# A decoder block whose FFN takes a plain product first: pair order, roots and scaling moved

## The chip, the cores and the metric

One core of a Trainium2 chip runs the whole kernel. The core has five engines with a queue each: TensorE (PE, matmuls), VectorE (DVE), ScalarE (ACT), GpSimd (POOL) and SyncE (SP), which issues most of the DMA transfers. Each engine takes its instructions strictly in the order of its queue and waits at semaphores for the others. The metric is the device time of one execution in microseconds (us), the median of several runs.

## The reference

The kernel computes one hybrid decoder block on a sequence of 1024 rows with 1024 columns in float32: a state-space branch and an attention branch, merged and multiplied by `w_o`, and then a gated FFN. The change touches the end of this and all of the FFN:

```python
merged = (jax.nn.sigmoid(gate_a) * y_a + jax.nn.sigmoid(gate_b) * y_b) @ w_o[l]
x = x + g1 * merged

h = modulate(rmsnorm(x, norm2_g[l]), sh2, sc2)
ffn = (jax.nn.silu(h @ w_ffn_gate[l]) * (h @ w_ffn_up[l])) @ w_ffn_down[l]
x = x + g2 * ffn
return rmsnorm(x, norm_f_g)
```

`rmsnorm` multiplies a row by one over the root of its mean square plus 1e-6. The hidden width of the FFN is 2816, that is 22 blocks of 128 or 11 pairs of blocks. The row g2 comes out of a small product of the conditioning vector with `w_ada`.

## The kernel before, in words

**Products.** A float32 product is made of three faster matmuls. Each operand is split into a rounded high part and the rest: `operand` (L462) copies it on ACT with a cast (L473, `wh`) and subtracts on DVE (L474, `wl`), and PE multiplies high by high, high by low and low by high (`PRODUCTS`). Where an operand is a sum of two blocks, the sum comes first (L471), on POOL or DVE. `pieces` makes the right operands of the FFN, out of the activations, and `next_ring` gives the slots of the left ones.

**The output projection, the norm and the transposes** (`attend_out`). For each of eight row tiles PE makes the product with `w_o`, DVE adds x, ACT sums the squares (L1148), `rstd` (L478 on) makes the root, ACT multiplies by it, and PE transposes (L1158) into four blocks of activations b11, b21 (row tiles 0 to 3) and b12, b22 (row tiles 4 to 7). `rstd` goes to and fro between two engines: a scale on DVE (L483), Ln and Exp on ACT (L486, L487), then a correction step in three DVE operations (L489, L493, L494), all on 128x1 elements.

**Gate and up** (`gate_up`, one call for each of the 11 pairs of hidden blocks). Each pair treats the gate weights and the up weights as two-by-two blocks and makes them by seven products instead of eight, in the order `ORDER = (2, 4, 5, 3, 1, 6, 7)`, one product of 12 matmuls for gate and one for up: 7 x 2 x 12 = 168 matmuls (L1255). Product 7 of the seven, for example, needs a sum of two weight blocks and the sum of b21 and b22. The right operands (seven of them, two tiles each) are made during pair 0 and kept. `combine` takes each product out of PSUM into four tiles `C` in slots `f1`: a copy on ACT for products 2 and 5 (L1262, L1266), adds on DVE for the others. PSUM has eight banks of 512 columns, named `tq`, `mm` and `wo` in the profile. At the end of a pair ACT applies Silu (L1235), DVE multiplies (L1236), and POOL makes five sums of the result (L1246), the left operands of the next product, which are stored to `hD` in DRAM. Product 2 of pair 1 is computed early, in the middle of pair 0 (the constant `N2`). Pair 10 goes last, and its result is stored as it is, in `lD`.

**Down** (`down`). Pairs 0 to 9 of the hidden blocks go through the seven-product form again, in three steps of four, three and three pairs (`STEPS`). For each step `weights` loads tiles of `w_ffn_down` into slots `pa` and POOL multiplies each by the row g2 (L1308). Then for each of the seven products the hidden sums are read back from `hD`, POOL adds two weight blocks (L1337), ACT and DVE split (L1334, L1335, L1338, L1339), PE multiplies (L1354), and DVE adds to seven accumulators `acc` (L1360). Four of these accumulators begin with blocks of x, and `acc[7]` is first corrected by `acc[5]` and `acc[4]`, four POOL operations (L1298) at the start of down. In the last step `closing` (L1315) sums the accumulators on POOL into the four result blocks. The two hidden blocks of pair 10 are multiplied last, plainly (L1394, 96 matmuls), and `close` makes the final norm of each row tile and stores it: squares on ACT (L1404, L1398), `rstd`, and a product of row, root and norm weight on DVE (L1379).

**What sets the order.** The program is written in order of the mathematics, with the waits put in by a framework that also sorts the instructions of every queue by its own estimate of when they can run. So the order on a queue is that of the built program and not always that of the text. A tile is a slot in a pool with a fixed number of buffers; a new tile waits until all who read the old one in its slot have done so. Calls of `after` fix one instruction behind another on the same engine, to keep ACT functions of one table together.

## Time and profile before

| what | us |
|---|---|
| median of 3 runs | 1496.89 (1492.9 to 1497.25) |
| the profiled execution | 1498.89 |
| its span, first to last instruction | 1497.2 |
| PE busy | 1414.6 |
| DVE busy | 1125.6 |
| ACT busy | 621.6 |
| POOL busy | 504.3 |

The mean granted clock of PE is 0.976 of full speed. A row of a timeline begins with its start and its length in us; x7 after it says that seven instructions alike stand in it. A bracket at its end gives how long the engine stood idle before it and who released it. In a group's row the busy time is followed by the mean of one in ns. Matmuls overlap: one of 512 columns is shown as 0.39 us, but they follow each other more closely than that.

### The profile page before, as it was taken

To read this page: it belongs to the slowest core of one execution; us is meant where nothing else is said; L and a number is where in the kernel's file an instruction comes from. 1 tells how busy PE (TensorE), PEld (TensorE's weight loads), DVE (VectorE), ACT (ScalarE), POOL (GpSimd) and SP (SyncE) were. 2 spreads that over 40 slices of the span, in tenths; PEclk is the share of its full clock that TensorE was granted. 3 is DMA by queue.
4 is the path that set the end of the run, shared out by engine and by line. 5 is a ranking of instruction groups with operands and counts; after the bars stand their busy time and mean duration, and the time that the engine had idled before them with its cause. 6 is when DMAs were issued, how large, how long until landed. Compare 5 with 4: busy or idle time off the path is not lost.

```text
span 1497.2 us, 18257 instructions
## 1 busy us (share of the span) xinstructions
PE 1414.6 (94%) x6706; PEld 1118.1 (75%) x6706; DVE 1125.6 (75%) x1523; ACT 621.6 (42%) x804; POOL 504.3 (34%) x266
## 2 busy tenths in 40 slices
PE   5898999999999999999998799999999998999995
PEld 3678888787666666668887588888888886888774
DVE  5878995456797989868637866666666669999997
ACT  3321122632587776764236433333333333433323
POOL 1000000102111111104300245444555468888795
PEclk9999999999999999999999899999999999999998
DMA  9556665579011112136533233333333346455312
GB/s 340 134 110 163 151 175 134 158 258 333 27 49 50 35 37 77 50 106 218 183 108 107 81 106 106 106 106 106 106 106 106 106 174 220 143 160 175 100 50 113
DMA packets 180409, 193.55 MB, mean 129 GB/s; under 512 B 28636, under 2 KB 130080, under 8 KB 180320
## 3 DMA queue, kind: packets, MB, share of 16 engines
q1 hardware_dynamic: 171184, 184.86, 39.3%
q10 hardware_dynamic: 8912, 7.48, 1.8%
q8 instruction: 53, 0.87, 0.2%
q14 instruction: 36, 0.29, 0.1%
q0 software_dynamic: 224, 0.05, 0.0%
HBM read 142.40 MB, written 48.76 MB: 128 GB/s over the span
## 4 chain that ended last, share of the span: by engine, by line
PE 61%; DVE 20%; issue 6%; DMA 5%; ACT 4%; POOL 3%; SPq 0%; DVEq 0%; ACTq 0%; POOLq 0%
PE tq L1255 11%; PE mm L1255 5%; PE wo L1255 5%; PE mx L807 5%; PE mm L807 4%; PE ga L733 4%; PE tq L1354 3%; PE acc L807 2%; PE mm L1112 2%; PE mm L641 2%; DMA aw<-in_w_ada_dram 2%; PE z L807 2%; PE wo L1112 2%; PE mm L733 2%; PE tq L1112 1%
## 5 line engine op out<-in xcount | busy, mean ns | idle before, releaser
L471 POOL TENSOR_TENSOR ws<-wb 128x1024 f32<-128x1024 f32 x26 | 64.2, 2470 | 181.1 <-PE tq L1158 78.1
L455 POOL TENSOR_TENSOR wl<-ws,wh 128x1024 fp32r<-128x1024 f32 x12 | 31.2, 2601 | 161.2 <-ACT wh L452 151.8
L900 DVE TENSOR_TENSOR wa<-wa,acc 128x512 f32<-128x512 f32 (+1 forms) x80 | 47.0, 628 | 32.6 <-ACT row L898 30.2
L1308 POOL TENSOR_TENSOR pa<-pa,row 128x1024 f32<-128x1024 f32 x22 | 64.1, 2939 | 2.2 <-DMA pa<-in_w_ffn_down_dram 2.2
L294 POOL MEMSET tz<- 128x1024 f32 x4 | 3.8, 953 | 179.4 <-PE mm L641 96.7
L1246 POOL TENSOR_TENSOR f<-f,f 128x512 f32<-128x512 f32 x30 | 50.0, 1693 | 31.4 <-DVE f L1236 22.9
L872 ACT ACTIVATE ws<-wa 128x1024 f32<-128x1024 f32 (+1 forms) x40 | 39.1, 976 | 48.5 <-DVE wa L869 43.3
L471 POOL TENSOR_TENSOR wgs<-wb 128x1024 f32<-128x1024 f32 x14 | 34.6, 2474 | 72.4 <-DVE wgl L474 30.3
L877 DVE TENSOR_TENSOR wl<-ws,wh 128x1024 fp32r<-128x1024 f32 (+1 forms) x40 | 57.1, 1427 | 1.0
L977 DVE SCALAR_TENSOR_TENSOR acc<-aw,cond,acc 128x512 f32<-128x512 f32 x56 | 43.8, 782 | 7.8 <-DMA aw<-in_w_ada_dram 6.9
L875 DVE SCALAR_TENSOR_TENSOR ws<-wa,ws 128x1024 f32<-128x1024 f32 (+1 forms) x40 | 45.5, 1136 | 4.9 <-ACT ws L874 3.9
L1354 PE MATMUL tq<-f,f 128*128 128x512 f32 x156 | 48.2, 390 | 0.2 <-DVE f L1339 0.2
L1235 ACT ACTIVATE f<-f 128x1024 f32<-128x1024 f32 x22 | 23.3, 1061 | 59.8 <-DVE f L1277 30.4
L903 ACT ACTIVATE wa<-wa 128x1024 f32<-128x1024 f32 (+1 forms) x40 | 38.8, 971 | 19.5 <-DVE wa L900 18.5
L452 ACT CAST wh<-ws 128x1024 fp32r<-128x1024 f32 x24 | 25.1, 1048 | 50.7 <-PE wo L1112 24.0
L807 PE MATMUL z<-q,k 64*128 64x512 f32 (+3 forms) x192 | 42.6, 534 | 3.7 <-DVE wa L869 2.6
L1337 POOL TENSOR_TENSOR wb<-pa 128x512 f32<-128x512 f32 x23 | 40.6, 1776 | 15.7 <-DVE wxl L1335 5.5
L454 POOL TENSOR_SCALAR wh<-ws 128x1024 fp32r<-128x1024 f32 x6 | 7.4, 1238 | 105.2 <-issue 36.1
L1246 POOL TENSOR_TENSOR f<-f 128x512 f32<-128x512 f32 x20 | 42.2, 2127 | 0.0
L807 PE MATMUL mm<-wa,V 128*64 128x512 f32 (+3 forms) x192 | 39.8, 507 | 0.0
L873 ACT ACTIVATE ws<-ws 128x1024 f32<-128x1024 f32 (+1 forms) x40 | 39.0, 974 | 1.1
L874 ACT ACTIVATE ws<-ws 128x1024 f32<-128x1024 f32 (+1 forms) x40 | 38.7, 968 | 0.3
(911 smaller groups left out, 4712.3 us busy)
## 6 DMA issues: line engine op xcount, KB each, us to landing
aw<-in_w_ada_dram SPq DMA_DIRECT2D x64, 256.0 KB, 4.6
hD<-f SPq DMA_DIRECT2D x30, 512.0 KB, 2.8
ws<-in_w_in_dram SPq DMA_DIRECT2D x23, 512.0 KB, 4.9
wb<-in_w_ffn_gate_dram SPq DMA_DIRECT2D x44, 256.0 KB, 4.2
wb<-in_w_ffn_up_dram SPq DMA_DIRECT2D x44, 256.0 KB, 4.5
pa<-in_w_ffn_down_dram SPq DMA_DIRECT2D x22, 512.0 KB, 5.1
wb<-hD SPq DMA_DIRECT2D x40, 256.0 KB, 2.8
x<-in_x_dram SPq DMA_DIRECT2D x16, 512.0 KB, 7.2
```

The lines of the kernel that those rows point to most:

```text
L471: (add or nc.gpsimd).tensor_tensor(st, a, b, op)
L733: self.nc.tensor.matmul(ps, lhsT=w[a][:, k], rhs=act[h][k][:, b], start=(j == 0), stop=(j == n - 1))
L807: return self.tc.keep_in_program_order(self.nc.tensor.matmul(*args, **kw))
L875: nc.vector.scalar_tensor_tensor(st, a, 0.0, st, ALU.max, ALU.add)
L877: nc.vector.tensor_tensor(lt, st, ht.bitcast(F32), ALU.subtract)
L900: nc.vector.tensor_tensor(a[:, x, 0:f], a[:, x, 0:f], r[:, x, 0:f], ALU.subtract)
L977: nc.vector.scalar_tensor_tensor(acc, w[:, j], cj, acc, ALU.mult, ALU.add)
L1112: self.nc.tensor.matmul(ps, lhsT=mg[t // 4][k][:, a, P * (t % 4):P * (t % 4) + P], rhs=ws[k // 2][b][:, k % 2], start=k + j == 0, stop=k + ...
L1246: nc.gpsimd.tensor_tensor(o, a, b, op)
L1255: self.nc.tensor.matmul(ps, lhsT=w[x][:, q, k], rhs=self.B[i](y, k), start=(j == 0), stop=(j == 11))
L1308: nc.gpsimd.tensor_tensor(w, w, g2, ALU.mult)
L1354: nc.tensor.matmul(ps, lhsT=o[x][:, P * t:P * t + P], rhs=o[y][:, R], start=(j == 0), stop=(j == 3 * np_ - 1))
```

## The change

1. Pair 10 is computed first instead of last, by the new function `plain`: an ordinary product with eight block products for each of gate and up, 192 matmuls. It uses b11 and b21 for row tiles 0 to 3, then b12 and b22 for 4 to 7, each as it is. `gate_up` then runs for ten pairs, and the early product of pair 1 is gone.
2. The roots of the second norm and of the final norm are made on ACT alone, by the new function `rstd_s`: Ln, Exp, two operations with a scale and a bias, two multiplications, all 128x1. A tile `eps` holds the constants.
3. The first eight tiles of `w_ffn_down` (`SCALED`) are loaded in the calls of pairs 2 to 9, multiplied by g2 on POOL, and stored in `wD`; `down` reads them from there in its first step. For this the row g2 is made after pair 1 instead of after pair 8.
4. The first step of down takes its products in the order `FIRST`, and the correction of `acc[7]` is issued when two products' operands have been issued.
5. `eps` has 19 columns where three are used, so that the tiles behind it begin at the same offset modulo 256 bytes as before.

The core of the diff:

```diff
-N2 = 3
+SCALED = 8
+FIRST = (2, 3, 1, 6, 7, 5, 4)
...
+    def rstd_s(self, ss, y, h, b=None):
+        act = self.nc.scalar.activation
+        b, bh = b or (self.eps[:, 0:1], self.eps[:, 1:2])
+        self.after(act(y, ss, AF.Ln, bias=b, scale=1.0 / 1024.0), self.fence)
+        self.root = act(y, y, AF.Exp, scale=-0.5)
+        act(h, ss, AF.Identity, bias=bh, scale=-0.5 / 1024.0)
+        self.nc.scalar.mul(h, h, y)
+        act(h, h, AF.Identity, bias=self.eps[:, 2:3], scale=y)
+        self.nc.scalar.mul(y, y, h)
         return y
...
+        self.eps = const.tile([P, 19], F32, name="eps")
+        for n, x in enumerate((1e-6, -0.5e-6, 1.5)):
+            self.after(nc.gpsimd.memset(self.eps[:, n:n + 1], x), self.fence)
...
-                r = self.rstd(const, ss, 1)
+                r = self.rstd_s(ss, *(const.tile([P, 1], F32, name=n, bufs=2) for n in ("r2", "h2")))
...
-                    self.B = {2: self.pieces(2, b11, None, self.PA, "pa"), 4: self.pieces(4, b21, b11, self.PA, "pa")}
+                    self.B = {2: self.pieces(2, b11, None, self.PA, "pa")}
+                    self.b21 = self.pieces(2, b21, None, self.PA, "pa")
...
-        for j in range(11):
+        w_v = i["w_ffn_down"][0].rearrange("(m p) n -> m p n", p=P)
+        self.plain(10, wv)
+        for j in range(10):
             self.gate_up(j, wv, tp)
-            if j == 8:
+            if j == 1:
                 g2 = self.rp.tile([P, 1024], F32, name="row")
                 self.ada_row(g2, 6, tp, self.banks, ("ft", None))
+            if 2 <= j < SCALED + 2:
+                t = tp.tile([P, 1024], F32, name="ft")
+                nc.sync.dma_start(out=t, in_=w_v[j - 2])
+                nc.gpsimd.tensor_tensor(t, t, g2, ALU.mult)
+                nc.sync.dma_start(out=self.wD[j - 2], in_=t)
+            if j == 8:
                 gf = tp.tile([P, 1024], F32, name="gf", bufs=1)
                 nc.scalar.dma_start(out=gf, in_=i["norm_f_g"].partition_broadcast(P))
         self.exp_ln(*self.silus)
         self.down(const, tp, g2, gf)
+    def plain(self, pair, wv):
+        nc = self.nc
+        b11, b12, b21, b22 = self.blocks
+        flat = lambda t: t.rearrange("p q k n -> p (q k n)")
+        w = {}
+        for x in range(2):
+            for y in range(2):
+                t = self.W.tile([P, 2, 4, P], F32, name="wb")
+                for q in range(2):
+                    nc.sync.dma_start(out=t[:, q], in_=wv[q][:, 4 * y:4 * y + 4, 256 * pair + P * x:256 * pair + P * x + P])
+                w[x, y] = [o.rearrange("p (q k n) -> p q k n", q=2, k=4) for o in self.operand(flat(t))]
+        parts = self.B[2], self.b21
+        us = [self.X.tile([P, 1024], F32, name="x1") for _ in range(2)]
+        for h in range(2):
+            if h:
+                parts = self.pieces(2, b12, None, self.PB, "pb"), self.pieces(5, b22, None, self.PB, "pb")
+                self.B[5] = parts[1]
+            for x in range(2):
+                ps = [self.banks.tile([P, 512], F32) for _ in range(2)]
+                for q in range(2):
+                    j = 0
+                    for y in range(2):
+                        for k in range(4):
+                            for a, b in PRODUCTS:
+                                nc.tensor.matmul(ps[q], lhsT=w[x, y][a][:, q, k], rhs=parts[y](b, k), start=j == 0, stop=j == 23)
+                                j += 1
+                g = self.X.tile([P, 1024], F32, name="x1")[:, 0:512]
+                self.after(nc.scalar.activation(g, ps[0], AF.Silu), self.root)
+                nc.vector.tensor_tensor(us[x][:, 512 * h:512 * h + 512], ps[1], g, ALU.mult)
+        for x in range(2):
+            nc.sync.dma_start(out=self.lD[x], in_=us[x])
...
-            if pair == 0 and n > 1:
+            if i not in self.B:
                 b11, b12, b21, b22 = self.blocks
-                if i not in self.B:
-                    u, v, pool, tag = {5: (b22, None, self.PB, "pb"), 3: (b12, b22, self.PB, "pb"), 1: (b11, b22, self.X, "x1"),
-                                       6: (b11, b12, self.X, "x1"), 7: (b21, b22, self.F, "f0")}[i]
-                    self.B[i] = self.pieces(i, u, v, pool, tag, Turns((tp, "ft")))
-            tiles = None
-            if pair == 0 and n < 2:
-                tiles = tuple(self.X.tile([P, 1024], F32R, name="x1") for _ in range(2))
-            if pair == 0 and n == N2:
-                raw = [self.X.tile([P, 2, 4, P], F32, name="x1") for _ in range(2)]
-                for y in range(2):
-                    for q in range(2):
-                        nc.sync.dma_start(out=raw[y][:, q], in_=wv[q][:, 4 * y:4 * y + 4, 256 + P:512])
-                w = self.operand(flat(raw[0]), flat(raw[1]), SIGN_A[2], tuple(self.X.tile([P, 1024], F32R, name="x1") for _ in range(2)),
-                                 nc.vector, nc.vector)
-                w = [t.rearrange("p (q k n) -> p q k n", q=2, k=4) for t in w]
-                self.M2 = tp.tile([P, 2, 512], F32, name="gf", bufs=1)
-                for q in range(2):
-                    ps = self.banks.tile([P, 512], F32)
-                    self.seven(ps, w, q, 2)
-                    nc.scalar.copy(self.M2[:, q], ps)
-            if pair == 1 and i == 2:
-                for q in range(2):
-                    M[q][2] = self.M2[:, q]
-                    self.combine(2, M[q], [None, None, None, C[q][1][:, 512:1024]])
-                continue
+                u, v, pool, tag = {4: (b21, b11, self.PA, "pa"), 3: (b12, b22, self.PB, "pb"), 1: (b11, b22, self.X, "x1"),
+                                   6: (b11, b12, self.X, "x1"), 7: (b21, b22, self.F, "f0")}[i]
+                self.B[i] = self.pieces(i, u, v, pool, tag, Turns((tp, "ft")))
             a, b = TERMS_A[i]
-            w = self.operand(flat(A[a]), b and flat(A[b]), SIGN_A[i], tiles, *(nc.vector if pair == 0 or (i, e) in AENG else nc.gpsimd for e in range(2)))
+            w = self.operand(flat(A[a]), b and flat(A[b]), SIGN_A[i], None, *(nc.vector if pair == 0 or (i, e) in AENG else nc.gpsimd for e in range(2)))
             w = [t.rearrange("p (q k n) -> p q k n", q=2, k=4) for t in w]
             for q in range(2):
                 ps = M[q][i] = self.banks.tile([P, 512], F32)
                 self.seven(ps, w, q, i)
                 self.combine(i, M[q], [C[q][0][:, 0:512], C[q][0][:, 512:1024], C[q][1][:, 0:512], C[q][1][:, 512:1024]])
-        if pair < 10:
-            self.silus = []
+        self.silus = []
...
-        for i, op in ((5, ALU.add), (4, ALU.subtract)):
-            for a in range(2):
-                nc.gpsimd.tensor_tensor(flat(acc[7][a]), flat(acc[7][a]), flat(acc[i][a]), op)
...
-            nc.sync.dma_start(out=w, in_=w_v[m])
-            nc.gpsimd.tensor_tensor(w, w, g2, ALU.mult)
+            if m < SCALED:
+                nc.sync.dma_start(out=w, in_=self.wD[m])
+            else:
+                nc.sync.dma_start(out=w, in_=w_v[m])
+                nc.gpsimd.tensor_tensor(w, w, g2, ALU.mult)
...
-            for n, i in enumerate(ORDER):
+            for n, i in enumerate(ORDER if s else FIRST):
+                if s == 0 and n == 2:
+                    for z, op in ((5, ALU.add), (4, ALU.subtract)):
+                        for a in range(2):
+                            nc.gpsimd.tensor_tensor(flat(acc[7][a]), flat(acc[7][a]), flat(acc[z][a]), op)
...
-                r = self.rstd(const, ss[:, 1:2], 1, ss[:, 0:1], at(t))
+                r = self.rstd_s(ss[:, 1:2], small[:, t, 2:3], small[:, t, 3:4], (small[:, t, 4:5], small[:, t, 5:6]))
-            r = self.rstd(const, ss[:, 0:1], 1, None, at(t))
+            r = self.rstd_s(ss[:, 0:1], small[:, t, 2:3], small[:, t, 3:4])
...
+                        for n, f in ((4, 1.0), (5, -0.5)):
+                            nc.scalar.activation(small[:, t, n:n + 1], ss[:, 0:1], AF.Identity, bias=self.eps[:, n - 4:n - 3], scale=f / 1024.0)
```

On PE's queue, where the output projection ends and gate and up begin (`x_6811`, `x_6939` and `wh`, `wl` are split weights, `pa` a right operand made of b11, `ident` the matrix for transposes); before:

```order
L1255 MATMUL wo<-pa,x_6812 128x512
L1255 MATMUL wo<-pa,x_6811 128x512
L1158 MATMUL tq<-ident,xh 128x128 x6
L1255 MATMUL wo<-pa,x_6811 128x512
L1255 MATMUL wo<-pa,x_6812 128x512
L1255 MATMUL mm<-pa,x_6939 128x512 x2
L1255 MATMUL wo<-pa,x_6939 128x512 x2
L1255 MATMUL mm<-pa,x_6940 128x512
```

and now:

```order
L1228 MATMUL wo<-pa,wh 128x512 x2
L1167 MATMUL tq<-ident,xh 128x128 x6
L1228 MATMUL wo<-pa,wl 128x512
L1228 MATMUL wo<-pa,wh 128x512 x2
L1228 MATMUL wo<-pa,wl 128x512
L1228 MATMUL wo<-pa,wh 128x512 x2
L1167 MATMUL tq<-ident,xh 128x128 x2
L1228 MATMUL wo<-pa,wl 128x512
L1228 MATMUL wo<-pa,wh 128x512 x2
```

The recursive product 2 of pair 0 and the early product behind it have given way to the plain product, whose weights lie in the ring's slots `wh` and `wl` instead of slots of x.

On POOL's queue, in pairs 1 to 4 (`ws<-wb` and `wgs<-wb` are sums of weight blocks, `f_...` the five sums of a pair's result); before:

```order
L471 TENSOR_TENSOR ws<-wb 128x1024 x2
L471 TENSOR_TENSOR wgs<-wb 128x1024
L471 TENSOR_TENSOR ws<-wb 128x1024
L1246 TENSOR_TENSOR f_7410<-f_7412,f_7413 128x512 x2
L1246 TENSOR_TENSOR f_7411<-f_7412,f_7413 128x512
L1246 TENSOR_TENSOR f_7412<-f_7412 128x512
L1246 TENSOR_TENSOR f_7413<-f_7413 128x512
L471 TENSOR_TENSOR wgs<-wb 128x1024
```

and now:

```order
L1270 TENSOR_TENSOR f_7389<-f_7391,f_7392 128x512 x2
L1270 TENSOR_TENSOR f_7390<-f_7391,f_7392 128x512
L1195 TENSOR_TENSOR ft<-ft,row 128x1024 x2
L472 TENSOR_TENSOR wgs<-wb 128x1024
L1270 TENSOR_TENSOR f_7391<-f_7391 128x512
L1270 TENSOR_TENSOR f_7392<-f_7392 128x512
L1195 TENSOR_TENSOR ft<-ft,row 128x1024
L472 TENSOR_TENSOR wgs<-wb 128x1024
L472 TENSOR_TENSOR ws<-wb 128x1024
L1195 TENSOR_TENSOR ft<-ft,row 128x1024
L472 TENSOR_TENSOR ws<-wb 128x1024
L1195 TENSOR_TENSOR ft<-ft,row 128x1024 x2
```

The rows of L1195 are the scaling multiplies. All eight stand within some 15 rows, from the middle of pair 1's five sums on, among the weight sums of the next two pairs, though the text issues one for each of pairs 2 to 9. On SP's queue their loads (L1194) and stores (L1196) stand there in turn, between weight loads of a pair and stores of sums:

```order
L1194 DMA ft<-in_w_ffn_down_dram 128x1024
L1273 DMA hD<-f_7392 128x1024
L1196 DMA wD<-ft 128x1024
L1194 DMA ft<-in_w_ffn_down_dram 128x1024
L1196 DMA wD<-ft 128x1024
L1243 DMA wb<-in_w_ffn_gate_dram 128x4x128
L1243 DMA wb<-in_w_ffn_up_dram 128x4x128
L1194 DMA ft<-in_w_ffn_down_dram 128x1024
L1196 DMA wD<-ft 128x1024
L1194 DMA ft<-in_w_ffn_down_dram 128x1024
```

Before, only weight loads and stores of sums stood on SP's queue in the pairs.

On POOL's queue, from the last of the gate and up pairs into down (`pa<-pa,row` is a multiply by g2, `pb<-pb` the correction, the rows into `ws`, `wgs`, `wb` from `pa` are sums of down weights); before:

```order
L1246 TENSOR_TENSOR f_9311<-f_9313,f_9314 128x512 x2
L1246 TENSOR_TENSOR f_9312<-f_9313,f_9314 128x512
L1246 TENSOR_TENSOR f_9313<-f_9313 128x512
L1246 TENSOR_TENSOR f_9314<-f_9314 128x512
L1308 TENSOR_TENSOR pa<-pa,row 128x1024 x4
L1337 TENSOR_TENSOR ws<-pa 128x512 x2
L1308 TENSOR_TENSOR pa<-pa,row 128x1024 x4
L1337 TENSOR_TENSOR wgs<-pa 128x512
L1337 TENSOR_TENSOR wb<-pa 128x512
L1298 TENSOR_TENSOR pb<-pb 128x1024 x4
L1337 TENSOR_TENSOR wgs<-pa 128x512
```

and now:

```order
L1364 TENSOR_TENSOR ws<-pa 128x512 x2
L1364 TENSOR_TENSOR wgs<-pa 128x512
L1364 TENSOR_TENSOR wb<-pa 128x512 x2
L1351 TENSOR_TENSOR pb<-pb 128x1024
L1364 TENSOR_TENSOR wb<-pa 128x512
L1351 TENSOR_TENSOR pb<-pb 128x1024 x2
L1364 TENSOR_TENSOR ws<-pa 128x512
L1351 TENSOR_TENSOR pb<-pb 128x1024
L1270 TENSOR_TENSOR f_9587<-f_9589,f_9590 128x512 x2
L1270 TENSOR_TENSOR f_9588<-f_9589,f_9590 128x512
L1364 TENSOR_TENSOR wb<-pa 128x512
L1364 TENSOR_TENSOR ws<-pa 128x512
```

The multiplies no longer stand here. The correction is threaded among the weight sums of the first products, and the five sums of pair 9 follow behind it.

More of the change, by code (lines that the diff above doesn't have):

```diff
@@ L475, in operand, with rstd @@
         return h, l
-    def rstd(self, pool, ss, n, more=None, at=None):
+    def rstd(self, pool, ss, n):
         nc = self.nc
-        v = at("v") if at else pool.tile([P, n], F32, name="rv")
-        y = at("y") if at else pool.tile([P, n], F32, name="ry")
-        a = at("a") if at else pool.tile([P, n], F32, name="ra")
-        nc.vector.tensor_scalar(v, ss if more is None else more, 1.0 / 1024.0, 1e-6, ALU.mult, ALU.add)
-        if more is not None:
-            nc.vector.scalar_tensor_tensor(v, ss, 1.0 / 1024.0, v, ALU.mult, ALU.add)
+        v, y, a = (pool.tile([P, n], F32, name=x) for x in ("rv", "ry", "ra"))
+        nc.vector.tensor_scalar(v, ss, 1.0 / 1024.0, 1e-6, ALU.mult, ALU.add)
         self.after(nc.scalar.activation(y, v, AF.Ln), self.fence)
         nc.scalar.activation(y, y, AF.Exp, scale=-0.5)
-        if n == 1:
-            nc.vector.scalar_tensor_tensor(a, y, v, y, ALU.mult, ALU.mult)
-        else:
-            nc.vector.tensor_tensor(a, y, y, ALU.mult)
-            nc.vector.tensor_tensor(a, a, v, ALU.mult)
+        nc.vector.tensor_tensor(a, y, y, ALU.mult)
+        nc.vector.tensor_tensor(a, a, v, ALU.mult)
         nc.vector.tensor_scalar(a, a, -0.5, 1.5, ALU.mult, ALU.add)
         nc.vector.tensor_tensor(y, y, a, ALU.mult)
+        return y
+    def rstd_s(self, ss, y, h, b=None):
[7 more added lines that the diff above has]
+        self.nc.scalar.mul(y, y, h)
         return y
@@ L1236, in gate_up @@
             nc.vector.tensor_tensor(u, u, g, ALU.mult)
-            if pair == 10:
-                nc.sync.dma_start(out=self.lD[x], in_=u)
-        if pair == 10:
-            return
         L, R = slice(0, 512), slice(512, 1024)
```

5 lines of the change are left out of this document (2 added, 3 removed).

## The prediction

> **What bounds the kernel now.** I read the page first, then the busy time by stretches, then PE's waits, and last the timelines around the two places where PE loses time.
>
> ```profile
> PE 1414.6 (94%) x6706; PEld 1118.1 (75%) x6706; DVE 1125.6 (75%) x1523; ACT 621.6 (42%) x804; POOL 504.3 (34%) x266
> PE 61%; DVE 20%; issue 6%; DMA 5%; ACT 4%; POOL 3%; SPq 0%; DVEq 0%; ACTq 0%; POOLq 0%
> ```
>
> The first line is busy time by engine, the second the chain of work that ended last. The kernel is PE-bound, and whatever PE does not lose cannot be won, unless the change removes matmuls. DVE's 20% of the chain says that it is DVE that makes PE wait where it waits. The next view has one row a stretch: its length, then each engine's busy time and instructions, the granted clock, the DMA share.
>
> ```profile
> 690.00:800.00 110.00, 110.00 (x509) 91.48 (x508) 61.83 (x87) 42.06 (x69) 25.79 (x13) 0.98 0.44 153
> 800.00:820.00 20.00, 15.73 (x75) 12.28 (x74) 20.00 (x26) 13.05 (x20) 0.00 (x0) 0.91 0.23 80
> 840.00:862.00 22.00, 11.92 (x41) 9.27 (x40) 22.00 (x23) 10.13 (x12) 3.20 (x1) 0.69 0.16 48
> 880.00:1160.00 280.00, 280.00 (x1237) 231.86 (x1236) 174.14 (x193) 86.40 (x98) 144.38 (x70) 1.00 0.33 107
> 1240.00:1260.00 20.00, 15.74 (x69) 12.35 (x67) 18.96 (x13) 4.47 (x7) 20.00 (x9) 1.00 0.61 223
> 1260.00:1280.00 20.00, 17.97 (x69) 14.69 (x70) 19.89 (x16) 12.94 (x19) 13.13 (x7) 0.83 0.43 141
> 1280.00:1300.00 20.00, 19.24 (x85) 15.60 (x85) 19.63 (x20) 6.86 (x7) 13.66 (x8) 1.00 0.56 175
> 1300.00:1360.00 60.00, 60.00 (x267) 49.69 (x266) 56.96 (x45) 24.28 (x32) 49.25 (x23) 1.00 0.47 142
> ```
>
> Columns of busy time are PE, weight load, DVE, ACT, POOL. Before 800 and from 880 to 1160 PE is full; at 800-820 and 840-862 DVE is full and PE starves, at 1240-1280 DVE and POOL are nearly full together and PE starves again. These PE rows mark the ends of the stages:
>
> ```profile
> 808.90 1.75 PE L1255 MATMUL wo<-pa,x 128*128 128x512 f32 x7
> 876.70 0.61 PE L1255 MATMUL wo<-pa,wh 128*128 128x512 f32 x2
> 1176.82 0.62 PE L1255 MATMUL wo<-pa,wh 128*128 128x512 f32 x2
> 1253.00 0.39 PE L1354 MATMUL tq<-wh 128*128 128x512 f32 x1
> 1480.38 0.39 PE L1394 MATMUL wo<-wh,wl 128*128 128x512 f32 x1
> ```
>
> They are the first gate/up matmul, the first of pair 1, the first of pair 9, the first down matmul and the last matmul. Pairs 9 and 10 are 336 matmuls in 1253.00 - 1176.82 = 76.18 us, so an undisturbed matmul costs 0.2267 us and a pair 38.1 us. From 808.90 to 876.70 PE did 168 matmuls of pair 0 and 24 of the early product of pair 1: 192 x 0.2267 = 43.5 us in 67.8, so 24.3 us went elsewhere (some of it the last transposes). From 1253.00 to 1480.77 it did 936: 212.2 us in 227.8, so 15.6 were lost. These 40 us and the 16.4 us from PE's end to the span's end are all that can be won.
>
> ```profile
> PE tq L1255 <- ACT f L1262: 10.1, 1, 10.1
> PE mm L1255 <- ACT x L473: 2.9, 1, 2.9
> PE mm L1255 <- DVE x L474: 1.4, 1, 1.4
> 852.43 2.35 DVE L471 TENSOR_TENSOR ft<-f,f 128x1024 f32<-128x1024 f32 x2
> 854.80 1.22 PE L1255 MATMUL tq<-pb,wh 128*128 128x512 f32 x2 [10.08 <-ACT f L1262]
> ```
>
> The 10.1 us stall is named after ScalarE's first result copy (L1262), but ScalarE is late itself: its target is an `f1` slot whose old content, the activations b21 and b22, DVE still reads for product 7's operand, as the last thing of its queue (the adds from 852.43 to 854.78). Eight PSUM banks fill meanwhile, PE stops, and two matmuls then take 1.22 us: the granted clock of that stretch is 0.69. So the stall is DVE's whole burst of making seven right operands, priced at 10.1 us of standing and some more of slow clock.
>
> **The plain pair first, and the roots.** The plain product needs no sums of activation blocks, only casts and differences (b11, b21, then b12, b22), and gives DVE 192 matmuls of cover before the first recursive pair asks for more. It costs 24 matmuls more than a pair of seven products: 24 x 0.2267 = +5.4 us, on the critical path. The early product of pair 1 goes; its 24 matmuls return in their own pair, at no cost. What is left of the 24.3 us is the question. Its first part lies with the roots:
>
> ```profile
> 811.88 0.14 DVE L483 TENSOR_SCALAR rv<-ss 128x1 f32<-128x1 f32 x1
> 815.42 0.20 ACT L487 ACTIVATE ry<-ry 128x1 f32<-128x1 f32 x1
> 818.28 0.22 DVE L489 SCALAR_TENSOR_TENSOR ra<-ry,rv 128x1 f32<-128x1 f32 x1
> 821.94 0.16 DVE L494 TENSOR_TENSOR ry<-ry,ra 128x1 f32<-128x1 f32 x1
> ```
>
> One 128x1 root takes from 811.88 to 822.10, 10.2 us for some 1.2 us of work, because each of its four DVE steps queues behind full-size operations. On ScalarE alone it is six operations near 0.2 us, some 1.4 us, threaded among the casts of one queue that is not full (13.05 of 20 us), and I let the last transposes come some 6 us earlier. From the queues I work out by hand, for the changed start: 1.4 us until the first weight cast, whose slot the output projection gives back only at its last matmul, 0.8 for the matching difference, 0.3 for the next, 2 for the transposes of the last two row tiles, then about 2.4 of slow clock and transposing: 6.9 us lost in place of 24.3. The plain pair and pair 0 then end at 808.9 + 360 x 0.2267 + 6.9 = 897.4; nine pairs (342.8) and the four small matmuls of the g2 row (0.9) end gate and up at 1241.1, against 1253.0: **-11.9**. Bounds: if only 3 us are lost, 24.3 - 5.4 - 3 = 15.9 gained; if only the 10.1 us stall goes, 10.1 - 5.4 = 4.7 gained. I stay nearer the first: pair 0's copies find their `f1` slots free some 4 to 8 us early by my count, since b21 and b22 are read during the plain pair.
>
> **Scaling during the pairs.** Eight multiplies leave the start of down:
>
> ```profile
> 1225.36 10.45 POOL L1308 TENSOR_TENSOR pa<-pa,row 128x1024 f32<-128x1024 f32 x4
> 1239.26 10.38 POOL L1308 TENSOR_TENSOR pa<-pa,row 128x1024 f32<-128x1024 f32 x4
> 1252.99 11.23 POOL L1298 TENSOR_TENSOR pb<-pb 128x1024 f32<-128x1024 f32 x4
> 987.80 4.71 POOL L1246 TENSOR_TENSOR f<-f,f 128x512 f32<-128x512 f32 x3 [1.90 <-DVE f L1236]
> L471 POOL TENSOR_TENSOR ws<-wb 128x1024 f32<-128x1024 f32 x21 | 50.4, 2401 | 85.8 <-DVE wl L474 49.3 <-DVE wgl L474 20.1 <-DVE wxl L474 16.3
> pa<-in_w_ffn_down_dram SPq DMA_DIRECT2D x22, 512.0 KB, 5.1
> hD<-f SPq DMA_DIRECT2D x30, 512.0 KB, 2.8
> ```
>
> They are 20.8 us of POOL, 2.6 each. In pairs POOL is busy 144.38 of 280 us, so there is room; the operand adds (L471, 2.4 us, three or four a pair) run about a pair ahead of PE. But the built order does not spread them over eight pairs: they stand together among the adds of pairs 3 and 4 and the sums of pairs 1 and 2, behind the g2 row, and on SP's queue eight loads and eight stores are threaded between the gate and up weights. Two buffers turn a load, a multiply and a store: 5.1 + 2.6 + 2.8 = 10.5 us per two tiles, if both are in flight. The six tiles after the first two are then 31.5 us, inside a pair's 38.1 of lead. I take +1.5 us for late adds or `hD` stores, bounds 0 and +8. The extra 8 MB lie under a DMA share of 0.33.
>
> **The transition.** The three stretches from 1240 to 1300 hold 69 + 69 + 85 = 223 matmuls where 60 us hold 264.7: 9.5 us lost, as the waits say:
>
> ```profile
> PE tq L1354 <- DVE wl L1335: 5.5, 1, 5.5
> L1335 DVE TENSOR_TENSOR wl<-pa,wh 128x512 fp32r<-128x512 f32 x3 | 5.3, 1764 | 0.0
> 809.00 1.22 DVE L474 TENSOR_TENSOR pa<-ws,pa 128x1024 fp32r<-128x1024 f32 x1
> ```
>
> The group row is of 1253-1300, with POOL beside it: 1.76 us for 128x512, while a difference twice as large takes 1.22 with POOL idle. Afterwards the multiplies are gone from here, the scaled tiles come back by DMA, and the correction stands behind two products' sums, so that the first operands are made before 1241. Then 2 to 3 us remain, since one operand slot is held by pair 9's last product: **-7**, bounds -9.5 and 0. Zero, because the four correction adds (11.2 us) and pair 9's five sums still fall in this stretch, now among the products' own sums, and DVE pays for each. The step-1 multiplies come later than before, eight in a row; I price that at nothing, since step 0's 336 matmuls cover 76 us, and PE is full in the next stretch, where they stand in part today; uncovered they would cost up to 8 x 2.6 = 21 us of POOL, less the lead.
>
> The Trainium skill ("SBUF — State Buffer", section "SBUF: two separate sides") has VectorE and GpSimd sharing a port pair as an exclusive lock held for a whole instruction, against a VectorE operation with two SBUF inputs. The rows above agree. By that rule alone the multiplies would block DVE as long among the pairs as here; the sum stays, since DVE has 106 of 280 us idle there.
>
> **The tail.** From PE's end (1480.77) to the span's end are 16.4 us, and it is DVE that is behind:
>
> ```profile
> 1468.46 1.04 DVE L494 TENSOR_TENSOR ss<-ss 128x1 f32<-128x1 f32 x1
> 1484.10 0.20 ACT L486 ACTIVATE ss<-ss 128x1 f32<-128x1 f32 x1 [1.17 <-DVE ss L483]
> 1492.18 0.75 DVE L1374 SCALAR_TENSOR_TENSOR pa<-pa,ss,gf 128x512 f32<-128x512 f32 x1
> ```
>
> A 128x1 step costs DVE up to 1.04 us beside POOL. Without four or five such steps a row DVE has two adds and a closing product left, about 2.7 us a row, as much as PE's 12 matmuls. Against that ScalarE's queue gets six steps a row, and the last two rows' roots stand behind each other. I take **-2.5**; bounds -5 (DVE's lag gone) and +1.5 (six steps where the DVE ones hid).
>
> The Trainium skill ("ScalarE: Activation LUTs", "Rules for kernel authors") sends `mul` and `add` to VectorE and budgets about 0.3 us for an ACTIVATE with a 128x1 pointer. By that figure a root would be 1.8 us, estimated, and the tail's gain near 2; the row shows 0.20, and the measured row decides.
>
> The eps tile's padding to 19 columns moves the left pools by 256 bytes in all, so every tile stands modulo 256 as it did, on both halves: nothing to pay or to win, cost 0. The three small POOL memsets run where POOL idles (0 of 20 us at 800-820).
>
> **Sum.** -11.9 + 1.5 - 7 - 2.5 = -19.9 against the profiled execution, whose time is 1498.89 (span 1497.2, 1.7 around it): 1479.0. The median of the runs, 1496.89, is 2.0 lower, so 1477.0.
>
> **Rivals.**
> *One of the two big gains fails* (1481 to 1490, about 1484). Either DVE stays full at the start, because the plain pair's own operands come from the same queue, and 14 us are lost in place of 6.9 (gain 4.7 in place of 11.9), or the transition's waits stay at 9.5. For: DVE is at 20.00 of 20 and 22.00 of 22 us at the start, and 18.96 and 19.89 of 20 at the transition. Against: the sums of blocks, two to a product at 1.2 us each, are what leaves the first stretch. Both failing together give 1491.
>
> *The bunched scaling throttles pairs 3 and 4* (slower, about 1502). If a store waits for its multiply at the head of SP's queue, and the next load and the weights of the next pair stand behind that store, the tiles go one after another: 6 x 10.5 = 63 us, 25 more than the 38.1 of lead, PE stands for these 25 and the clock falls after. It decides from 38.1 / 6 = 6.4 us a tile. For: the built SP order really has store, load, store, load in turn between weight loads. Against: two buffers, and POOL's other work in those pairs waits for DVE, not for SP (the releasers of L471).
>
> *It does not do what it says* (within 0.3%): the padding keeps an alignment that was already there, and if alignment were what mattered nothing moves; the other parts would have to cancel.
>
> **Chances.** The forecast (1470 to 1481) 0.57, more than it (below 1470: no loss at all at either place) 0.05, one gain failing 0.22, both failing or cancelling 0.06, the throttle 0.10. About 0.3% (4.5 us) is what a measurement of this kernel can tell from no change: faster 0.84, same 0.06, slower 0.10. The range 1466 to 1492 holds the first four but their edges; the slower side is left out with 0.10.
>
> **What would show it.** Right: PE busy throughout 840-862, no wait on the copy into `f1`; gate/up's last matmul near 1243; the transition's PE waits at 3 us or less; the last matmul near 1463; some 14 us from there to the end. Wrong: PE waits inside pairs 2 to 4 on POOL's L471 successors or on gate and up loads (the throttle), a wait in the plain pair's second half on DVE, or down's first step again waiting for `wl`.

## The result and the profile after

The changed kernel takes 1487.33 us, the median of 7 runs (1481.03 to 1490.7), against 1496.89 for the kernel before (7 runs, 1490.46 to 1498.83). The ratio is 0.9936, with a 95% interval from 0.992 to 0.9952: some 9.6 us faster, between 7 and 12. The prediction had the direction, and its range held the time, but the gain is half of what its sum said (19.9). The two profiled executions, which the rows below are from, took 1498.89 and 1484.92 us, 2.0 above the one median and 2.4 below the other, so they lie 14.0 us apart.

The page of the changed kernel, busy time by engine and the chain that ended last:

```profile
PE 1414.1 (95%) x6730; PEld 1118.0 (75%) x6730; DVE 1106.2 (75%) x1444; ACT 634.8 (43%) x867; POOL 499.9 (34%) x265
PE 62%; DVE 17%; issue 6%; DMA 6%; ACT 5%; POOL 2%; SPq 0%; DVEq 0%; ACTq 0%; POOLq 0%
```

The first stretch is mended, the second is not. Busy time by stretches, in the columns of before (PE, weight load, DVE, ACT, POOL, clock, DMA share, and GB/s moved):

```profile
800.00:820.00 20.00, 16.91 (x80) 12.35 (x79) 15.23 (x19) 18.89 (x35) 0.00 (x0) 0.96 0.52 157
820.00:840.00 20.00, 20.00 (x79) 16.14 (x79) 9.69 (x10) 5.80 (x7) 0.00 (x0) 0.87 0.17 53
840.00:862.00 22.00, 22.00 (x99) 18.23 (x98) 12.24 (x12) 7.89 (x9) 0.00 (x0) 1.00 0.15 48
1240.00:1260.00 20.00, 17.68 (x78) 14.33 (x77) 19.89 (x12) 8.09 (x9) 20.00 (x9) 1.00 0.26 76
1260.00:1280.00 20.00, 16.77 (x64) 12.72 (x64) 15.62 (x10) 7.83 (x9) 18.84 (x11) 0.91 0.57 176
1300.00:1360.00 60.00, 57.77 (x254) 47.23 (x253) 60.00 (x54) 21.23 (x27) 46.51 (x21) 1.00 0.52 160
```

At 840-862 PE is full where it did 11.92 of 22 us. At 1240-1280 it did 142 matmuls where before it did 138, though down begins 10.8 us earlier now; POOL is nearly full there (20.00 and 18.84 of 20), DVE in the first half (19.89). And at 1300-1360, where PE was full before, DVE is full now and PE does 254 matmuls in place of 267. These PE rows mark the stages: the first plain matmul, the first of pair 0, the first of down, the last:

```profile
806.23 0.74 PE L1228 MATMUL wo<-pa,wh 128*128 128x512 f32 x2
860.51 0.62 PE L1279 MATMUL wo<-pa,wh 128*128 128x512 f32 x2
1242.24 0.39 PE L1381 MATMUL mm<-wh 128*128 128x512 f32 x1
1469.18 0.39 PE L1418 MATMUL tq<-wh,wl 128*128 128x512 f32 x1
```

| stage, us | before | after | change | predicted |
|---|---|---|---|---|
| gate and up, first matmul to down's first | 444.1 | 436.0 | -8.1 | -11.9 + 1.5 |
| down, first to last matmul | 227.8 | 227.3 | -0.5 | -7 |
| last matmul to the end of the span | 16.4 | 13.6 | -2.8 | -2.5 |

The spans differ by 14.0 us; the other 2.7 of it lie ahead of all of this, in a part that the change does not touch and whose end stands between 804.4 and 811.1 in the profiles of this study. So stages are compared by their lengths below. Each is of one execution: in the eight kernels with the new roots the tail, which is the same code in all, takes 11.5 to 13.6 us, and the first stretch, from the first plain matmul to the first of pair 0, 50.9 to 54.6, so a length is uncertain by some 2 us.

What PE waited for from 800 to the end, in the changed kernel (total, times, longest; the six largest):

```profile
PE mm L1381 <- DVE wxl L1366: 2.7, 2, 2.2
PE tq L1381 <- ACT f L1365: 2.5, 1, 2.5
PE tq L1418 <- DVE wl L475: 2.4, 1, 2.4
PE mm L1381 <- DVE wgl L1362: 2.3, 1, 2.3
PE tq L1167 <- ACT f L1173: 1.6, 1, 1.6
PE tq L1228 <- DVE f L1171: 1.0, 1, 1.0
```

The 10.1 us on the copy into `f1` are gone, no wait inside the pairs is left, and four of six stand in down (L1381, L1418). The 2.2 us in the first row fall in the stretch from 1300 to 1360:

```profile
1307.26 12.40 POOL L1331 TENSOR_TENSOR pa<-pa,row 128x1024 f32<-128x1024 f32 x4 [2.29 <-DMA pa<-in_w_ffn_down_dram]
1320.79 0.50 PE L1381 MATMUL mm<-wxl,wxh 128*128 128x512 f32 x1 [2.23 <-DVE wxl L1366]
```

POOL multiplies the tiles of down's second step there, beside DVE, and PE then waits for DVE's difference.

### The profile page after: what moved, and what is told of

Same layout as the page of the kernel before. It is cut to its first block, busy times and chain, and to the rows that moved or that the text cites. A ratio compares the mean times of both kernels' runs of the same rounds, so it can differ in the third digit from the quotient of the medians.

```text
span 1483.2 us, 18301 instructions
## 1 busy us (share of the span) xinstructions
PE 1414.1 (95%) x6730; PEld 1118.0 (75%) x6730; DVE 1106.2 (75%) x1444; ACT 634.8 (43%) x867; POOL 499.9 (34%) x265
## 4 chain that ended last, share of the span: by engine, by line
PE 62%; DVE 17%; issue 6%; DMA 6%; ACT 5%; POOL 2%; SPq 0%; DVEq 0%; ACTq 0%; POOLq 0%
PE tq L1279 13%; PE wo L1279 6%; PE mm L1279 6%; PE mx L813 5%; PE mm L813 4%; PE ga L739 4%; PE acc L813 2%; PE mm L647 2%; PE mm L1118 2%; DMA aw<-in_w_ada_dram 2%; PE z L813 2%; PE tq L1228 2%; PE wo L1118 2%; PE mm L739 2%; PE tq L1118 1%
## 5 line engine op out<-in xcount | busy, mean ns | idle before, releaser
L1270 POOL TENSOR_TENSOR f<-f,f 128x512 f32<-128x512 f32 x30 | 52.5, 1778 | 20.4 <-DVE f L1264 11.9
L1381 PE MATMUL tq<-f,f 128*128 128x512 f32 x156 | 48.3, 394 | 0.3 <-DVE f L1366 0.3
L472 POOL TENSOR_TENSOR wgs<-wb 128x1024 f32<-128x1024 f32 x12 | 29.8, 2483 | 46.1 <-DVE wxl L475 23.1
L1331 POOL TENSOR_TENSOR pa<-pa,row 128x1024 f32<-128x1024 f32 x14 | 42.2, 3041 | 3.5 <-DMA pa<-in_w_ffn_down_dram 3.5
L475 DVE TENSOR_TENSOR wl<-ws,wh 128x1024 fp32r<-128x1024 f32 x20 | 29.0, 1448 | 18.1 <-ACT wh L474 18.0
L879 ACT ACTIVATE ws<-ws 128x1024 f32<-128x1024 f32 (+1 forms) x40 | 39.0, 974 | 1.1
L1279 PE MATMUL tq<-pa,wh 128*128 128x512 f32 x128 | 39.4, 389 | 0.0
```

The lines of the kernel that those rows point to most:

```text
L472: (add or nc.gpsimd).tensor_tensor(st, a, b, op)
L1270: nc.gpsimd.tensor_tensor(o, a, b, op)
L1279: self.nc.tensor.matmul(ps, lhsT=w[x][:, q, k], rhs=self.B[i](y, k), start=(j == 0), stop=(j == 11))
L1331: nc.gpsimd.tensor_tensor(w, w, g2, ALU.mult)
L1381: nc.tensor.matmul(ps, lhsT=o[x][:, P * t:P * t + P], rhs=o[y][:, R], start=(j == 0), stop=(j == 3 * np_ - 1))
```

## The experiments

The first runs ask what down's start waits for, the next what each part of the change is worth alone, the last what a version with all of it in the pairs does.

**No scaling during the pairs.**

```diff
-SCALED = 8
+SCALED = 0
-            if j == 1:
+            if j == 8:
```

> Edit: no weight tile is scaled during the pairs; all 22 multiplies by g2 stand in down again, and the g2 row is made after pair 8. All else as in the changed kernel. Theory A (the moved multiplies do relieve the start of down, and the correction with pair 9's sums took the room): gate and up unchanged within 1 us, down longer by 4 to 9 us, total slower by 4 to 9 us. Theory B (moving them bought nothing there, since DVE is blocked by whatever POOL does in that place): down within 2 us of the changed kernel's 227.4, total within 2 us.

Measured: 1493.93 us, ratio to before 0.9977 (0.9963 to 0.9991). Down is 237.2 us. So theory A: moving eight multiplies is worth 6.6 us by the medians and some 10 in down's length. (Gate and up are 3.3 us shorter than in the changed kernel, against the "unchanged within 1 us"; all of that lies in the plain pair's stretch, 50.9 us, and the pairs take 381.7 in both.) But that left a riddle: without scaling, down is 9.4 us longer than before the change. Something else in the change had taken as much as the scaling gave.

**The correction later**, and **no correction at all.**

```diff
-                if s == 0 and n == 2:
+                if s == 0 and n == 5:
```

> Edit: the correction of acc[7] is issued behind five products of down's first step in place of two. Theory A (the correction's 11.4 us of POOL ahead of pair 9's five sums keep the f1 slots taken and block DVE): the wait of PE on ACT's copy into f (2.5 us) and most of the 7.7 us lost from 1240 to 1280 go; down 3 to 6 us shorter than 227.4. Theory B (the same 11.4 us of POOL block DVE wherever they stand, and meet the eight late multiplies there): down within 2 us, with the loss moved to 1290 to 1330.

```diff
-                if s == 0 and n == 2:
-                    for z, op in ((5, ALU.add), (4, ALU.subtract)):
-                        for a in range(2):
-                            nc.gpsimd.tensor_tensor(flat(acc[7][a]), flat(acc[7][a]), flat(acc[z][a]), op)
```

> Leaves out the correction of acc[7] altogether, so one of four blocks of the result lacks it; the time is a lower bound for any place of these four operations. Theory A: down 4 to 8 us shorter than 227.4. Theory B (the transition's waits are the weights' and hidden sums' own: two products' operands and pair 9's sums): within 2 us.

Later: 1488.12 us, ratio 0.9944 (0.9925 to 0.9963), down 228.8: theory B, no gain. Left out: 1478.96, ratio 0.988 (0.9858 to 0.9901), down 222.1: 8.4 us below the changed kernel by the medians, 5.3 in down's length. The four operations cost PE 5 to 8 of their own 11 us, and their place hardly matters. The timeline of POOL in the changed kernel at the start of down shows what stands together there (the weight sums between these rows are not shown):

```profile
1241.54 6.21 POOL L1351 TENSOR_TENSOR pb<-pb 128x1024 f32<-128x1024 f32 x2
1249.93 2.80 POOL L1351 TENSOR_TENSOR pb<-pb 128x1024 f32<-128x1024 f32 x1
1252.70 6.19 POOL L1270 TENSOR_TENSOR f<-f,f 128x512 f32<-128x512 f32 x3
1264.78 3.49 POOL L1270 TENSOR_TENSOR f<-f 128x512 f32<-128x512 f32 x2
```

and this is what stands beside it on DVE and ACT:

```profile
1227.93 0.69 DVE L1362 TENSOR_TENSOR wxl<-pa,wxh 128x512 fp32r<-128x512 f32 x1
1250.45 2.83 DVE L1362 TENSOR_TENSOR wgl<-pa,wgh 128x512 fp32r<-128x512 f32 x1
1264.34 1.04 ACT L1365 CAST f<-wgs 128x1024 fp32r<-128x1024 f32 x1 [7.79 <-DMA hD<-f]
```

Pair 9's five sums (L1270) come at 1252.70 to 1268.27, 10 to 26 us after down has begun. In the kernel before they lie 36 us ahead of it, under pair 10's matmuls:

```profile
1217.22 4.71 POOL L1246 TENSOR_TENSOR f<-f,f 128x512 f32<-128x512 f32 x3 [1.91 <-DVE f L1236]
```

The late sums hold the `f1` slots: ACT idles 7.79 us until they have been stored to `hD`, and PE has its wait on `f` (2.5 us). And the 128x512 differences on DVE that run beside a POOL operation take 1.7 to 2.8 us where the same form took 0.69 at 1227.93, with POOL idle as it began. The Trainium skill ("SBUF — State Buffer", "SBUF: two separate sides") calls this an exclusive lock between VectorE and GpSimd, and the row agrees. This gave theory C: pair 10 at the end had been the cover for POOL's work, and the plain pair first takes it away. "Cover" means here matmuls under which another engine's work makes nobody wait.

**The plain pair alone**, all other parts undone; its first form stood at other offsets in memory (see the last section), so it was run again with `eps` widened.

```diff
-SCALED = 8
+SCALED = 0
-                r = self.rstd_s(ss, *(const.tile([P, 1], F32, name=n, bufs=2) for n in ("r2", "h2")))
+                r = self.rstd(const, ss, 1)
...
-            for n, i in enumerate(ORDER if s else FIRST):
+            for n, i in enumerate(ORDER):
```

> Edit: of the changed kernel only the plain pair first is left; roots on both engines, all multiplies in down, the correction at down's front and the old order of products are as in the kernel before. Theory C (pair 10 at the end was the cover under which POOL made pair 9's five sums and eight multiplies; taken away, down starts late): gate and up 436 to 441 us, against 444.3 before; down 236 to 245, against 227.8; total 1493 to 1502, no faster than before. Theory D (the plain pair costs the start of down nothing, and the new order with the correction among its products costs the 9.5 us that the run without scaling showed): down 226 to 230, total near 1489.

> Edit: as the run with the plain pair alone (1509.97 us), with eps at 51 columns, so that both halves stand at 224 modulo 256. Theory E: pairs back from 387.5 to 381.8 us, total 1502 to 1506: still slower than before, because down stays at 235 to 237 (pair 9's sums and the eight multiplies without pair 10 as cover). Theory F: 1508 to 1512.

Measured: 1509.97 us, ratio 1.0088 (1.0068 to 1.0108), and with the offsets of before 1501.76, ratio 1.0032 (1.0017 to 1.0048). The first is slower than theory C had it (1493 to 1502); the last section has the reason. Alone, the plain pair makes the kernel slower by some 5 us: gate and up are 3.9 us shorter (440.4 against 444.3, both counted from here on from the last matmul of the output projection to down's first), down is 7.9 longer (235.7). POOL in this kernel, aligned:

```profile
1220.62 11.44 POOL L1342 TENSOR_TENSOR pa<-pa,row 128x1024 f32<-128x1024 f32 x4
1248.71 12.78 POOL L1329 TENSOR_TENSOR pb<-pb 128x1024 f32<-128x1024 f32 x4
1261.45 5.60 POOL L1277 TENSOR_TENSOR f<-f,f 128x512 f32<-128x512 f32 x3
```

Multiplies, correction and pair 9's sums stand in one row, the sums last, 16 us after down's first matmul (1245.3). The multiplies have found other cover, pair 9's own matmuls; the sums have none.

**The scaling on the kernel before**, and **the correction at the front again** on the changed kernel.

```diff
+            if 2 <= j < SCALED + 2:
+                t = tp.tile([P, 1024], F32, name="ft")
...
+            if m < SCALED:
+                nc.sync.dma_start(out=w, in_=self.wD[m])
```

> Edit: the kernel before, with the eight tiles scaled during pairs 2 to 9 and g2 made after pair 1, and nothing else; pair 10 stays last. Theory C: the multiplies' removal gains its full price where pair 10 still covers pair 9's sums: down 217 to 222 against 227.8, gate and up within 2 us of 444.3, total 1487 to 1491. Theory D (the multiplies were not what PE waited for): down 226 to 230, total within 2 us of before.

```diff
-                if s == 0 and n == 2:
...
-            for n, i in enumerate(ORDER if s else FIRST):
+            for n, i in enumerate(ORDER):
```

> Edit: the changed kernel with the correction at down's front again and the old order of products in its first step; plain pair, roots and scaling stay. Theory C: down 228 to 236, a little longer than the changed kernel's 227.4, since the four operations stand ahead of the first weight sums. Theory D: down 217 to 222.

The first takes 1498.14 us, ratio 0.9996 (0.998 to 1.0012), with down at 222.5; the second 1484.96, ratio 0.9918 (0.9898 to 0.9937), with down at 230.3. Theory C had down's length in both (222.5 is half a us above its range), and missed the first one's total, 1487 to 1491. Lengths of down, all with the old order and the correction at the front (the last one, 230.3, with the new roots, the others with the old):

| down, us | eight multiplies in down | scaled during the pairs |
|---|---|---|
| pair 10 last | 227.8 (before) | 222.5 |
| pair 10 first | 235.7 | 230.3 |

The cover is worth 7.9 and 7.8 us, the scaling 5.3 and 5.4: two effects that add up. Since the cover is worth as much without the eight multiplies as with them, it is not their cover that is missed; by the rows above it is that of pair 9's sums, though no run leaves the sums out to show it. The new order with the correction behind two products takes the last one to 227.3 in the profiles, but the medians go the other way (1484.96 and 1487.33, with overlapping intervals), so that part is not shown to be worth anything.

Why did scaling on the kernel before gain nothing? Gate and up there are 5.8 us longer, and these rows of POOL and ACT explain most of it:

```profile
961.49 3.38 POOL L1185 TENSOR_TENSOR ft<-ft,row 128x1024 f32<-128x1024 f32 x1
964.82 5.75 POOL L1254 TENSOR_TENSOR f<-f,f 128x512 f32<-128x512 f32 x3
974.82 0.59 ACT L1270 COPY f<-tq 128x512 f32<-128x512 f32 x1 [13.61 <-DMA hD<-f]
```

The copy of a product waits 13.61 us for a store of the pair before; its sums (L1254) stand behind scaling multiplies (L1185) on POOL's queue, and PE stands 4.3 us. That is akin to the throttle of the rivals, by way of POOL's queue and in another kernel than the one that it was named for: in the changed kernel PE waits nowhere in its pairs.

**The roots on DVE and ACT again**, first at other offsets, then aligned.

```diff
-                r = self.rstd_s(ss, *(const.tile([P, 1], F32, name=n, bufs=2) for n in ("r2", "h2")))
+                r = self.rstd(const, ss, 1)
-            r = self.rstd_s(ss[:, 0:1], small[:, t, 2:3], small[:, t, 3:4])
+            r = self.rstd(const, ss[:, 0:1], 1, None, at(t))
```

> Edit: the changed kernel with all late roots on DVE and ACT in turn again, at both places. If the roots are worth what the prediction gave them: from the last matmul to the end 15 to 17 us against the changed kernel's 13.6, gate and up 1 to 4 us longer than 436.2. If they hide: both within 1 us.

> Edit: as the run with the late roots on DVE and ACT in turn (1501.92 us), but with eps widened to 51 columns, which puts the left pools back to the same offset modulo 256 bytes as the right ones (224); in that run they stood at 96. Theory E (the offsets cost about 1% on each matmul of the pairs, 387.3 us from the first recursive matmul to down's first against 381.7): these 5.6 us go; roots alone then cost 4 to 6 us at the plain pair and 2 to 4 at the end, total 1492 to 1497. Theory F (the offsets do nothing and the roots cost all 14 us): total stays at 1500 to 1504.

1501.92 us, ratio 1.0032 (1.0016 to 1.0049), and aligned 1494.77, ratio 0.9987 (0.9972 to 1.0003). At other offsets gate and up came out 10 us longer than the changed kernel's (446.4) where 1 to 4 were expected; aligned they are 4 longer (440.4). So the roots themselves are worth 7.4 us of the medians: gate and up 440.4 with the old ones against 436.3, and 14.6 against 13.6 us at the end. Over all profiles the tail takes 14.6 to 16.4 us in the six kernels with the old roots and 11.5 to 13.6 in the eight with the new ones.

**The width of `eps`.**

```diff
-        self.eps = const.tile([P, 19], F32, name="eps")
+        self.eps = const.tile([P, 3], F32, name="eps")
```

> Edit: the tile eps has the 3 columns that are used in place of 19, so the pools on the left of memory begin at other offsets modulo 256 bytes. Theory A (the offset changes nothing that the kernel is bound by): total within 2 us of the changed kernel. Theory B (two inputs at different offsets modulo 256 cost DVE or POOL time): the mean of the 128x1024 difference on DVE rises over 1.22 us or the sum on POOL over 2.40, and the total is slower by 5 us or more.

and the same with 51 columns:

> Edit: the changed kernel with eps at 51 columns in place of 19 and nothing else, so its left pools stand at 96 modulo 256 bytes against 224 on the right. Theory E: the pairs take 386 to 388 us in place of 381.7, down 0 to 3 us longer, total 5 to 10 us slower than the changed kernel (1492 to 1497). Theory F: within 2 us of 1487.3.

With 3 columns 1488.16 us, ratio 0.9951 (0.9934 to 0.9968), with 51 columns 1491.27, ratio 0.9965 (0.9944 to 0.9986), a little below the expected 1492 to 1497. Neither time alone is told surely from the changed kernel's; the stage lengths are: from the first recursive matmul to down's first 385.9 and 387.3 us, against 381.7. Of the three columns' two theories neither named PE, and it is PE's matmuls that became slower. The last section has the rows.

**All of it in the pairs.** The table and the run without correction pointed to a better version: take every multiply and the correction out of down, and hold each behind its pair's five sums, so that none of them bunch.

```diff
-            if 2 <= j < SCALED + 2:
+            for m in range(3 * (j - 2), min(3 * (j - 1), SCALED)) if j > 1 else ():
...
-                nc.gpsimd.tensor_tensor(t, t, g2, ALU.mult)
+                self.after(nc.gpsimd.tensor_tensor(t, t, g2, ALU.mult), self.sums)
...
+            if j in (2, 3):
...
```

The last lines left out load three blocks of x for each half, add one, subtract one, and store what `acc[7]` begins with.

> Edit: on the changed kernel, all 22 down tiles are scaled during the pairs, three to a pair, each held behind that pair's five sums so that they do not bunch, and the corrected first block of acc[7] is made there too (from the same sums, stored and loaded). Down then has no multiply and no correction on POOL. Theory A/C (each us of POOL in down costs PE most of a us, since DVE is full there; the correction alone was worth 8 us): down 214 to 219 against 227.4, pairs 0 to 4 us longer, total 1472 to 1480. Rival (POOL and the stores now throttle the pairs): pairs 10 us longer or more, total 1485 or more.

1471.16 us, ratio 0.9825 (0.9801 to 0.985): 26 us faster than before, 16 faster than the changed kernel. Gate and up 434.4 (436.3 in the changed kernel), down 215.5 (of 212.2 that its matmuls need), 11.5 at the end. Its stretches, and its waits of PE from 800 on:

```profile
900.00:1160.00 260.00, 260.00 (x1149) 215.34 (x1148) 199.55 (x183) 78.70 (x90) 189.31 (x82) 1.00 0.55 181
1240.00:1300.00 60.00, 57.56 (x253) 46.85 (x252) 53.48 (x44) 27.09 (x35) 43.78 (x22) 1.00 0.68 233
1300.00:1360.00 60.00, 60.00 (x267) 49.69 (x266) 51.95 (x55) 23.56 (x30) 26.45 (x17) 1.00 0.55 176
PE tq L1387 <- DVE f L1372: 2.3, 1, 2.3
PE tq L1167 <- ACT f L1173: 1.7, 1, 1.7
PE tq L1238 <- DVE f L1171: 0.5, 1, 0.5
```

POOL is busy 189 of 260 us in the pairs, DVE 200, and PE is full there: what blocks DVE costs nothing where DVE has room. At 1300-1360 it is full again, with no multiply beside it. Not all work has left down's start, though: two of the multiplies still run there, at 1243.15 and 1263.77, and so do pair 9's five sums, the first three of them here:

```profile
1249.17 5.62 POOL L1280 TENSOR_TENSOR f<-f,f 128x512 f32<-128x512 f32 x3 [1.16 <-DVE f L1274]
```

PE loses 3.1 us in the first 312 matmuls of down all the same, against 11.1 in the changed kernel. So the sums alone do not cost 8 us; they do so beside the correction, in the kernels of the table. The run changed three things at once (the other multiplies, the correction, the hold behind the sums), and what each is worth was not measured.

## Why the prediction was right or wrong

**The first stretch**, -11.9: mechanism right, size off. The 10.1 us stall vanished, as did the wait on the `f1` slots, and the pairs ran without loss (381.7 us for 1680 matmuls and four small ones). The loss that was left was put at 6.9 us and measured 54.28 - 43.53 = 10.75; in the profiles of the eight kernels with the new roots it is 7.4 to 11.1, above 6.9 in all. Three things stand out in the trace. The slow clock: the 15 matmuls from 819.12 to 825.54 took 6.4 us in place of 3.4 (the granted clock of 820-840 is 0.87), after PE had waited three times in the 5 us ahead; I had 2.4 for this and the transposing together. The roots are dearer on ACT than the 0.20 us that I took, and an instruction that I never priced stands in the way:

```profile
810.16 0.37 ACT L499 ACTIVATE h<-h,eps,r 128x1 f32<-128x1 f32 x1
814.40 1.28 ACT L1231 ACT_TABLE_LOAD   x1
815.70 0.60 ACT L1231 ACTIVATE x<-wo 128x512 f32<-128x512 f32 x1
816.19 1.93 ACT L1173 ACTIVATE f<-tq,mod,G 128x256 f32<-128x256 f32 x4
```

The steps with 128x1 scales and biases take 0.28 to 0.39 us. The figure of the Trainium skill ("ScalarE: Activation LUTs", "Rules for kernel authors", about 0.3 us with a pointer operand) was the better one, and the row that I preferred was of a simpler instruction. And the plain pair's first Silu, with its table load, is queued between the last roots and the copies out of the transposes, which come 1.9 us later for it; PE waits 1.6 us for just these. Of the 8.1 us of gain in this stage some 4 are the plain pair's and some 4 the roots'; I had seen the roots as a small part of one sum. That gate and up ended at 1242, close to the 1243 that I gave as a sign, is luck: the stage began 2.7 us earlier than in the old profile.

**Scaling in the pairs**, +1.5: 0 in the changed kernel. The bunching did no harm there, and 4.3 us of standing on the kernel before.

**The transition**, -7: this is the step that failed. It reads "the multiplies are gone from here", and "Then 2 to 3 us remain". Over down's first 216 matmuls PE lost 10.2 us before and 8.4 now (216 x 0.2267 taken off the time that they took): -1.8, and 8.4 us remain in place of 2 to 3. As forecast, the first product's 24 matmuls now run without loss, where 9.1 us went before; the loss has moved to the next ones.

The multiplies' own price was close (5.3 to 5.4 of down measured, 6.6 by the medians of the run without scaling). What failed is the base from which it was taken off: I counted the 9.5 us lost in the kernel before and subtracted, as if the rest of that stretch stayed. But the first part of the change takes pair 10's 38 us of matmuls from between pair 9 and down, and under them POOL had made pair 9's sums and then all eight multiplies (by the prediction's own rows, 1225.36 to 1249.64, ahead of down's first matmul at 1253.00). The multiplies then fall under pair 9's matmuls; the sums fall into down, onto the correction. I named those sums as something that "still fall in this stretch" and used them as a bound; in the kernel before they did not fall there at all. Moving a piece of work has a price at the place that it leaves: here 7.9 us, beside the correction. So 7.9 - 5.4 - 3.0 (from 230.3 to 227.3, the new order or the luck of one execution; the medians don't show it) = -0.5 stands in place of -7.

A smaller term failed with it: the step-1 multiplies, "I price that at nothing". With four of them on POOL beside DVE, PE stands 2.23 us at 1320.79 and loses 2.5 over 48 matmuls (the 265th to the 312th of down), where the kernel before lost none and the version with all of it in the pairs, without these multiplies, loses none. The rival "one of the two big gains fails" came out in its number (1481 to 1490) and in its condition (the transition's waits stay, with DVE full beside POOL); that the sums lose their cover, it did not say.

**The tail**, -2.5: -2.8, right. With the old roots, aligned, it is 14.6 in place of 13.6; over all profiles the two kinds of kernel don't overlap, and lie some 3 us apart in the mean.

**The padding**, 0: right, since it keeps the offsets equal. What it saves shows only in the runs at other offsets: 4 to 6 us in the pairs.

**The throttle** (0.10): not in the changed kernel; something akin to it, at 4.3 us of standing in place of 25, on the kernel before.

## What to carry to other kernels

When work moves from the end of a stage to its beginning, list what other engines did under it where it stood, and price that list without its cover; a loss read from the old profile is a loss under the old cover. Where DVE and POOL fill a stretch together, POOL's two-input work costs PE time, though not its full length: eight multiplies ahead of down (20.8 us of POOL) cost 5 us, the correction in it (11 us) 5 to 8. So it pays to move such work to where DVE has room, and to move all of it: eight multiplies gained 5 us of down's length (235.7 to 230.3), 22 and the correction 20 (to 215.5, with the new order and roots).

## What the runs showed of the hardware that I had not expected

In these kernels a matmul is slower when its two operands begin at different offsets modulo 256 bytes. The offsets are those of the built program, and no trace shows them; but the edits of `eps` shift the left pools by 128 bytes (51 columns for 19) and by -64 (3 for 19). With `eps` at 51 columns, the slots of the left pools (`pa`, `pb`, `wh`, `wgh`) begin at 96 modulo 256 and those of the right ones (`x`, `f`, `wxh`) at 224; in the kernel before, and in the changed one, all begin at 224. PE rows of that run, each the first of 24 matmuls, the third the first after them:

```profile
1024.16 0.62 PE L1279 MATMUL tq<-pa,wgh 128*128 128x512 f32 x2
1029.61 0.64 PE L1279 MATMUL mm<-pb,wxh 128*128 128x512 f32 x2
1035.20 0.62 PE L1279 MATMUL wo<-pb,wh 128*128 128x512 f32 x2
```

Left with left: 5.45 us for 24, 0.2271 each. Left with right: 5.59 us, 0.2329 each. Over 900 to 1220 of this run, from one matmul's start to the next, high and low parts taken together, the kinds of equal offset stand at 0.2269 to 0.2285 us (`pb` with `wh` 0.2269, `x` with `wxh` 0.2277), those of unequal offset at 0.2323 to 0.2333 (`x` with `wh` and `pa` with `wxh` 0.2329); in the changed kernel all twelve kinds stand at 0.2267 to 0.2268. It is not the clock: in this stretch the granted clock is 1.00 in both, with 1394 matmuls here and 1413 in the changed kernel. The ten recursive pairs take 387.3, 387.3 and 387.5 us in the three kernels at 96, 385.9 in the one at 160, and 381.7 to 382.8 in the eight changed ones at 224. Nothing waits in the trace for these 5.6 us, and they would have been charged to the roots (14.6 us in the run that was not aligned, 7.4 in the one that was). Why the offsets matter, no run here shows.
